# Low parts of the weights: half of the tiles on GpSimd, or all on the vector engine

## The chip, the cores and the metric

The kernel runs on one core of one Trainium2 chip. The metric is device microseconds of one execution, from the chip's own timer; several executions are given by their median.

## What is computed

One step of a hybrid decoder layer on a prompt of 2048 tokens and a sample group of 8 x 8 tokens with the same weights, all in float32. From the reference, cut:

```python
h = rmsnorm(x, norm1_g)
proj = h @ w_in                                   # 1024 -> 36 x 128 columns
q, ka, va, rw, gates = jnp.split(proj, [...], axis=-1)
att = attn_fn(q, ka, va)                          # window 128, sinks, bias
rw_out = rwkv7_mixer(rw, ...)                     # matrix state, token by token
g_a, g_b = jnp.split(jax.nn.sigmoid(gates), 2, axis=-1)
x = x + (g_a * (att @ w_pa) + g_b * (rw_out @ w_pb)) @ w_o
ug, uv = jnp.split(rmsnorm(x, norm2_g) @ w_up, 2, axis=-1)
x = x + (jax.nn.gelu(conv3(ug)) * uv) @ w_down    # inner width 2816
```

## The kernel before

**Products in two parts.** A float32 product is made of three matmuls in the faster type fp32r: each operand is split into a high part (the value cast to fp32r) and a low part (the value minus the high part), and high x high, high x low and low x high are summed in PSUM. `gemm` (L471 on) does this for one 128-column block of the weights: for each of 8 (or 4, 6) row blocks k the pairs (whi, xh), (whi, xl), (wlo, xh).

**The weights.** `load_w` loads a tile of 128 x 8 x 128 raw weights by a DMA on SP's queue (L358). `split_w` makes its parts in two halves: ScalarE (ACT) casts a half to `whi` (L383), then `wsub` (L424) subtracts it into `wlo`. `wsub` numbers its calls and sends every second one to GpSimd (POOL), the others to the vector engine (DVE). Since a tile has two halves, its first goes to DVE and its second to POOL. Raw, high and low tiles take turns in one ring of 7 buffers (`W_SLOTS`), three to a tile, so weights are made about two tiles ahead.

**First phase** (`phase1`, to about 1450 us): the tokens in six groups of up to 384. Each group runs 36 blocks of `w_in`, and attention and the RWKV scan as background processes between the blocks. The first three groups split `w_in` tiles and write the parts back to memory (L369), a third of the tiles in each; later passes load the parts (L353). So three groups make 72 tiles, 144 halves. In `gemm`, the halves of a coming tile are issued after k = 1 and k = 5 (`W_AT`). The lane solve (L1032, L1034) is a chain of 60 small DVE operations per group. The order of PE's instructions is written out by hand here, from a model of the time; the order of the other queues is left to the framework's scheduler.

**Second phase** (`phase2`): three groups of 704 tokens, each in two chunks of 352 columns. Per group: `w_ab` and `w_o` (8 tiles each), then the FFN in four parts of 4, 6, 6 and 6 blocks: up-projections (`w_ug`, `w_uv`, one tile each a block), and 8 tiles of `w_down` a part. That is 276 tiles, 552 halves. All queues, PE's too, are ordered by the scheduler, which weighs instructions by costs of its own. L1320 and L1323 make low parts of activations on DVE; L1386 and L1449 are POOL's products and sums of activations; L1333 sums squares; L1339, L1381, L1382 and L1397 are loads on POOL's queue.

`nopool` keeps halves off POOL at the turn of the two phases, and `last_load` ties the next POOL half behind POOL's loads of `outs`.

Of the kernel before, what the change touches and what calls it, by code (L numbers as in the profile page):

```python
# [78 lines left out]
Y_rwkv_post_1 = 1505  # L79
Y_rwkv_post_2 = 1205  # L80
W_AT = (1, 5)
W_POOL = (2, 0)
W_AHEAD, W_SPLIT, W_SLOTS = 2, 2, 7
P_SM = P_SW = P_T2 = 0
P_H = 1
# [86 lines left out]
class Build:  # L172
# [1322 lines left out]
    def run(self):  # L1495
        cfg = self.cfg
        self.pool_every = W_POOL[0]
        self.wnext = self.bg = None
# [112 lines left out]
```

## Time and profile before

| | |
|---|---|
| median of 3 runs | 3415.2 us (3404.68 to 3422.92) |
| the profiled execution, its own time | 3414.19 us |
| its span, first to last instruction | 3412.4 us |
| busy PE, DVE, ACT, POOL | 3274.9, 1941.7, 1162.7, 1106.6 us |
| mean granted PE clock | 0.975 of full speed |

The profile is of one execution. A row of the timeline gives start and length in us, engine, line, operation, what is written and read, the shape, and in brackets how long the engine sat idle before it and what ended that. A line named L424 is line 424 of the kernel. PE's matmuls overlap, so their lengths are about twice their distance.

### The profile page before, as it was taken

Reading aid. Unit: us, or ns where it says so; the run is one execution under the profiler, and the core shown is the slowest. Engines: PE = TensorE matmul, PEld = TensorE weight load, DVE = VectorE, ACT = ScalarE, POOL = GpSimd, SP = SyncE. Lnnn points to the kernel's source line nnn. Section 1 sums busy time; section 2 is a strip of 40 time slices with the busy share of each in tenths; the row PEclk is TensorE's granted clock in tenths of the full one; section 3 lists DMA queues with packets and bytes.
Section 4 is the critical chain, followed back from the end, with each engine's and each line's share of the span. In section 5 each row is a group of like instructions: output and inputs, shape, how many; then the busy total and the mean of one; then the engine's idle time right before and its main releaser. Section 6 shows DMA issues by size and latency. Waiting matters only on the chain.

```text
span 3412.4 us, 59346 instructions
## 1 busy us (share of the span) xinstructions
PE 3274.9 (96%) x23574; PEld 3124.1 (92%) x23574; DVE 1941.7 (57%) x3658; ACT 1162.7 (34%) x2370; POOL 1106.6 (32%) x1242
## 2 busy tenths in 40 slices
PE   7899999989999999899999999999999999999998
PEld 6879888878888889799999999999999999999998
DVE  6764775664664765655454465555464655564564
ACT  4444443332333333223232233332232323232232
POOL 4333432321221222152233332423243342343342
PEclk9989989899999999999999999999999999999999
DMA  5446467684565658562222224512222352222222
GB/s 174 147 142 228 162 204 240 214 267 151 195 197 191 211 181 287 170 217 68 64 70 72 67 63 130 172 59 77 70 66 72 97 181 74 63 70 73 68 69 74
DMA packets 197069, 460.22 MB, mean 135 GB/s; under 512 B 62719, under 2 KB 95111, under 8 KB 196791
## 3 DMA queue, kind: packets, MB, share of 16 engines
q1 hardware_dynamic: 169367, 396.33, 36.0%
q0 software_dynamic: 8704, 37.78, 3.3%
q10 hardware_dynamic: 18720, 22.31, 1.8%
q8 instruction: 185, 3.03, 0.4%
q14 instruction: 93, 0.76, 0.1%
HBM read 377.03 MB, written 79.31 MB: 134 GB/s over the span
## 4 chain that ended last, share of the span: by engine, by line
PE 78%; DVE 9%; DMA 6%; ACT 3%; issue 2%; POOL 2%; SPq 0%; ACTq 0%; DVEq 0%; POOLq 0%
PE acc L287 69%; PE ps L287 5%; DMA w<-w_in 2%; PE psA L287 2%; DVE LN L1034 1%; DVE TX L1032 1%; POOL wlo L424 1%; ACT whi L383 1%; PE psY L287 1%; ACT at L778 1%; DMA gates<-raw 1%; POOL th L1386 1%; DVE wlo L424 1%; DVE at L768 0%; DMA raw<-x 0%
## 5 line engine op out<-in xcount | busy, mean ns | idle before, releaser
L287 PE MATMUL acc<-A,whi 128*128 128x352 f32 x4992 | 1008.6, 323 | 3.8 <-DVE A L1320 3.1
L287 PE MATMUL acc<-h,whi 128*128 128x384 f32 (+2 forms) x3456 | 899.2, 340 | 14.3 <-DVE h L588 4.1
L287 PEld LDWEIGHTS acc<-A,whi 128*128 128x128 f32 x4992 | 837.3, 188 | 5.4 <-DVE A L1320 4.0
L424 POOL TENSOR_TENSOR wlo<-w,whi 128x512 fp32r<-128x512 f32 (+2 forms) x347 | 477.2, 1376 | 1070.4 <-ACT whi L383 977.9
L383 ACT CAST whi<-w 128x512 fp32r<-128x512 f32 (+2 forms) x696 | 373.6, 581 | 1066.9 <-PE acc L287 496.9
L287 PEld LDWEIGHTS acc<-h,whi 128*128 128x128 f32 x3456 | 621.8, 194 | 47.0 <-issue 15.1
L287 PE MATMUL acc<-A,wlo 128*128 128x352 f32 x2496 | 605.7, 324 | 0.0
L287 PE MATMUL acc<-B,whi 128*128 128x352 f32 x2880 | 582.5, 323 | 4.6 <-ACT B L1322 2.4
L287 PE MATMUL acc<-h,wlo 128*128 128x384 f32 (+2 forms) x1728 | 581.0, 336 | 1.4 <-DMA wlo<-w_in_lo 1.0
L287 PEld LDWEIGHTS acc<-B,whi 128*128 128x128 f32 x2880 | 481.9, 188 | 6.4 <-DVE B L1323 3.3
L424 DVE TENSOR_TENSOR wlo<-w,whi 128x512 fp32r<-128x512 f32 (+2 forms) x349 | 302.8, 868 | 256.8 <-ACT whi L383 244.4
L287 PEld LDWEIGHTS acc<-A,wlo 128*128 128x128 f32 x2496 | 435.4, 188 | 0.1
L287 PE MATMUL acc<-B,wlo 128*128 128x352 f32 x1440 | 350.2, 323 | 0.0
L287 PEld LDWEIGHTS acc<-h,wlo 128*128 128x128 f32 x1728 | 334.3, 193 | 15.0 <-issue 3.6
L287 PEld LDWEIGHTS acc<-B,wlo 128*128 128x128 f32 x1440 | 250.9, 188 | 0.0
L1478 DVE TENSOR_TENSOR x<-x,acc 128x352 f32<-128x352 f32 x188 | 89.3, 516 | 227.2 <-PE acc L287 227.2
L1449 POOL TENSOR_TENSOR ss<-ss,ssq 128x704 f32<-128x704 f32 x66 | 113.2, 1715 | 297.2 <-DVE ss L1448 264.0
L1437 DVE SCALAR_TENSOR_TENSOR cc<-ub,vt,cc 128x704 f32<-128x704 f32 (+1 forms) x132 | 145.9, 1105 | 37.4 <-ACT cc L1431 35.6
L1427 DVE TENSOR_TENSOR ub<-acc,ssq 128x352 f32<-128x352 f32 (+1 forms) x132 | 61.5, 507 | 117.5 <-PE acc L287 116.2
L1323 DVE SCALAR_TENSOR_TENSOR B<-ss,B 128x704 fp32r<-128x704 f32 x66 | 113.4, 1718 | 4.0 <-ACT B L1322 3.9
L1445 ACT ACTIVATE ss<-cc 128x704 f32<-128x704 f32 x66 | 52.4, 793 | 162.4 <-DVE cc L1437 110.5
L619 ACT COPY raw<-acc 128x384 f32<-128x384 f32 (+1 forms) x84 | 37.4, 445 | 168.4 <-PE acc L287 164.1
(302 smaller groups left out, 3605.9 us busy)
## 6 DMA issues: line engine op xcount, KB each, us to landing
whi<-w_in_hi SPq DMA_DIRECT2D x144, 512.0 KB, 4.6
wlo<-w_in_lo SPq DMA_DIRECT2D x144, 512.0 KB, 3.9
w<-w_in SPq DMA_DIRECT2D x72, 512.0 KB, 4.5
w<-w_ug SPq DMA_DIRECT2D x66, 512.0 KB, 3.5
w<-w_uv SPq DMA_DIRECT2D x66, 512.0 KB, 3.5
w<-w_down SPq DMA_DIRECT2D x72, 384.0 KB, 3.1
w_in_hi<-whi SPq DMA_DIRECT2D x36, 512.0 KB, 2.7
w_in_lo<-wlo SPq DMA_DIRECT2D x36, 512.0 KB, 5.3
```

Of the source, the lines that this page charges most:

```text
L287: self.pe(self.nc.tensor.matmul(out, lhsT, rhs, start=start, stop=stop), max(n * (1 if rhs.dtype == F32R else 4) / 2.4, 25))
L383: nc.scalar.copy(out=hi[:, a:b], in_=w[:, a:b])
L424: i = eng.tensor_tensor(**kw)
L619: nc.scalar.copy(out=raw[:, 1:1 + n], in_=acc[:, :n])
L778: nc.scalar.activation(out=t[:, h, :], in_=t[:, h, :], func=AF.Exp, bias=nm[:, h:h + 1], accum_out=su[:, h:h + 1])
L1032: nc.vector.tensor_tensor(out=tv, in0=LN[:NL, j:j + 1, j + 1:32].broadcast_to([NL, j, w]), in1=LN[:NL, 0:j, j:j + 1].broadcast_to([NL, j, ...
L1323: nc.vector.scalar_tensor_tensor(out=lo[:, :T], in0=src[:, :T], scalar=scale, in1=hi[:, :T].bitcast(F32), op0=MUL, op1=SUB)
L1427: nc.vector.tensor_tensor(out=ub[:, 2 + a:2 + e], in0=pp[:, :e - a], in1=rs[:, a:e], op=MUL)
L1437: nc.vector.scalar_tensor_tensor(out=cc[:, :n], in0=ub[:, j:j + n], scalar=self.v(wn, f), in1=cc[:, :n], op0=MUL, op1=ADD)
L1445: nc.scalar.activation(out=s[:, :T], in_=cc[:, :T], func=AF.Square, scale=GELU_A)
L1449: nc.gpsimd.tensor_tensor(out=s[:, :T], in0=s[:, :T], in1=rs[:, :T], op=MUL)
L1478: nc.vector.tensor_tensor(out=x2[m][:, a:b], in0=x2[m][:, a:b], in1=pp[:, :b - a], op=ADD)
```

## The change

The period with which halves go to POOL becomes 2^30 in place of 2, so that none does.

```diff
 W_AT = (1, 5)
-W_POOL = (2, 0)
+W_POOL = (1 << 30, 0)
 W_AHEAD, W_SPLIT, W_SLOTS = 2, 2, 7
```

The first number is `pool_every` in `wsub`; the second isn't used:

```python
eng = self.nc.gpsimd if self.wn % self.pool_every == 0 and not self.nopool else self.nc.vector
i = eng.tensor_tensor(**kw)
if eng is self.nc.gpsimd and self.last_load:
    self.tc.add_manual_dep(i.ins, self.last_load, ORDER, reason="loads first")
```

Since no half is on POOL, the tie to `last_load` falls away too. ACT's casts, the loads and the matmuls are the same.

## Rows read from the trace of the kernel before

**Rows 1.** The page, busy us of each engine, share of the span, instructions.
```profile
PE 3274.9 (96%) x23574; PEld 3124.1 (92%) x23574; DVE 1941.7 (57%) x3658; ACT 1162.7 (34%) x2370; POOL 1106.6 (32%) x1242
```
**Rows 2.** PE's waits, whole span: us in total, times, longest.
```profile
PE psA L287 <- DVE at L806: 14.6, 9, 5.2
...
PE ps L287 <- DVE G L1004: 7.0, 4, 3.3
PE acc L287 <- DVE ssq L1333: 7.0, 2, 3.8
...
PE acc L287 <- ACT B L1322: 2.4, 1, 2.4
...
PE acc L287 <- DVE wlo L424: 0.3, 2, 0.2
```
**Rows 3.** Busy time by stretch: start:end, length; PE, PEld, DVE, ACT, POOL; clock, DMA.
```profile
150.00:180.00 30.00, 24.57 (x132) 23.98 (x131) 28.62 (x86) 11.15 (x28) 6.85 (x6) 0.89 0.52 165
...
1600.00:1800.00 200.00, 200.00 (x1239) 200.00 (x1238) 109.38 (x142) 61.80 (x101) 66.33 (x59) 1.00 0.22 65
...
2110.00:2117.00 7.00, 6.93 (x27) 6.90 (x28) 2.77 (x16) 0.00 (x0) 0.00 (x0) 0.51 0.22 75
...
2400.00:2600.00 200.00, 200.00 (x1252) 200.00 (x1252) 98.13 (x131) 57.11 (x93) 64.83 (x54) 1.00 0.23 69
```
**Rows 4.** Groups by line and shape: count, busy us, mean ns, idle before them.
```profile
L424 POOL TENSOR_TENSOR wlo<-w,whi 128x512 fp32r<-128x512 f32 x251 | 370.8, 1477 | 724.7 <-ACT whi L383 684.7 <-ACT vt L723 14.4 <-DMA w_in_lo<-wlo 10.4
...
L424 DVE TENSOR_TENSOR wlo<-w,whi 128x512 fp32r<-128x512 f32 x253 | 239.4, 946 | 195.4 <-ACT whi L383 183.6 <-ACT vt L723 7.7 <-PE acc L287 1.8
...
L1323 DVE SCALAR_TENSOR_TENSOR B<-ss,B 128x704 fp32r<-128x704 f32 x66 | 113.4, 1718 | 4.0 <-ACT B L1322 3.9
...
L424 POOL TENSOR_TENSOR wlo<-w,whi 128x384 fp32r<-128x384 f32 x72 | 88.2, 1226 | 262.8 <-ACT whi L383 210.4 <-DVE x L1478 44.0 <-PE acc L287 8.4
```
**Rows 5.** The tile wlo: ns min/median/max, first and last start, main forms.
```profile
L424 POOL TENSOR_TENSOR wlo<-w,whi x347: 732/1313/2292, 18.7 to 3375.8; 128x512 fp32r<-128x512 f32 x126, 128x384 fp32r<-128x384 f32 x36, 128x256 fp32r<-128x256 f32 x12
```
**Rows 6.** Timeline of DVE, then of POOL, second phase, 1669 to 1681 us.
```profile
1669.13 0.43 DVE L424 TENSOR_TENSOR wlo<-w,whi 128x256 fp32r<-128x256 f32 x1 [1.64 <-ACT whi L383]
...
1678.81 0.69 DVE L424 TENSOR_TENSOR wlo<-w,whi 128x512 fp32r<-128x512 f32 x1 [3.56 <-ACT whi L383]
...
1679.44 1.29 POOL L424 TENSOR_TENSOR wlo<-w,whi 128x512 fp32r<-128x512 f32 x1 [4.91 <-ACT whi L383]
```
**Rows 7.** Timeline of DVE, then of POOL, in the first group's lane solve.
```profile
161.33 0.40 DVE L1034 TENSOR_TENSOR LN<-LN,TX 96x234 f32<-96x234 f32 x1
161.76 1.38 DVE L1032 TENSOR_TENSOR TX<-LN 96x238 f32<-96x238 f32 x1
...
161.51 1.36 POOL L424 TENSOR_TENSOR wlo<-w,whi 128x512 fp32r<-128x512 f32 x1 [3.86 <-ACT whi L383]
```
**Rows 8.** Timeline of POOL, then of DVE, before PE's stop at 2182 us.
```profile
2178.36 1.27 POOL L424 TENSOR_TENSOR wlo<-w,whi 128x512 fp32r<-128x512 f32 x1 [0.71 <-ACT whi L383]
2179.60 2.11 POOL L1386 TENSOR_TENSOR th<-th 128x704 f32<-128x704 f32 x1
...
2182.57 0.89 DVE L1323 SCALAR_TENSOR_TENSOR B<-th,B 128x704 fp32r<-128x704 f32 x1 [2.38 <-ACT B L1322]
```
**Rows 9.** Timeline of DVE at 66 us, first group.
```profile
66.56 0.69 DVE L424 TENSOR_TENSOR wlo<-w,whi 128x512 fp32r<-128x512 f32 x1 [3.76 <-ACT whi L383]
67.17 2.04 DVE L1004 TENSOR_TENSOR G<-ps,ct 128x512 f32<-128x512 f32 x4
```
**Rows 10.** The tile wlo on PE from 1660 to 1692 us (columns as rows 5).
```profile
L287 PE MATMUL acc<-A,wlo x20: 322/324/325, 1682.7 to 1691.6; 128*128 128x352 f32 x20
```
**Rows 11.** Timeline of POOL and DVE at a group end, then of DVE at the end.
```profile
2108.00 1.27 POOL L424 TENSOR_TENSOR wlo<-w,whi 128x512 fp32r<-128x512 f32 x1 [4.93 <-ACT whi L383]
...
2108.59 1.42 DVE L1333 TENSOR_TENSOR ssq<-ssq,ss 128x704 f32<-128x704 f32 x1 [0.52 <-ACT ss L1332]
...
3382.44 0.89 DVE L1333 TENSOR_TENSOR ssq<-ssq,ss 128x704 f32<-128x704 f32 x1 [0.92 <-ACT ss L1332]
```

## The prediction

> **What bounds the kernel now.** I read the busy times first: TensorE (PE) is busy 96% of the span, the vector engine (DVE) 57%, GpSimd (POOL) 32% [rows 1]. So the next question was what PE waited for. All of PE's idle time is 137.5 us (3412.4 - 3274.9), in many small pieces, and the reader is to see in the waits how little of it comes from what the change touches: low parts made by DVE ended 0.3 us of PE's waits in the whole span, and none made by POOL stands in that list [rows 2]. The larger pieces are DVE results of other kinds: the scores' mask L806, the masked products L1004, the sums of squares L1333 [rows 2]. Last the busy time by stretch: in the second phase PE doesn't stop for whole stretches, 200.00 of 200 us at full clock [rows 3]. There the floor is PE's own pace.
>
> **What is taken away and what is added.** POOL makes 251 halves of 128x512 and 72 of 128x384 [rows 4], 347 in all [rows 5]; the other 24 are of 128x256. All go to DVE. Alone, a DVE half takes 0.69 us for 512 columns and 0.43 us for 256 [rows 6]; for 384 I take 0.56, midway. The sum: 251 x 0.69 + 72 x 0.56 + 24 x 0.43 = 173.2 + 40.3 + 10.3 = 224 us more on DVE.
>
> Part of it comes back, because DVE is slow beside POOL. A product in the lane solve takes 0.40 us on DVE; the one that starts 0.25 us after a POOL half takes 1.38 us, and ends just after that half's 1.36 us are over [rows 7]. So a POOL half costs a busy DVE some 1.0 us, and an idle one nothing: 0 to 347 us in all. Between these ends I take what the two groups lose that lose most: DVE's own halves of 512, 253 x (0.946 - 0.69) = 65 us [rows 4, 6], and the activations' low parts L1323, 66 x (1.718 - 0.89) = 55 us [rows 4, 8]. Some of these 120 us belong to other POOL work, and other groups lose a little too. DVE then has 1942 + 224 - 120 = 2046 us, 60% of the span; from end to end 1819 to 2166 us, 53% to 63%. POOL falls from 1107 to about 630 us. Over the span no end of this makes DVE the bound; what counts is where PE stands behind DVE.
>
> **On PE's path, first phase.** Only the first three groups of tokens split weights; later ones read the parts back. DVE's fullest stretch is 150 to 180 us, the lane solve of the first group: 28.62 of 30 us [rows 3]. At its end PE waits 5.2 us for L806 [rows 2], which stands in DVE's queue behind the chain. Three POOL halves fall in the stretch, of which the rows show one, each costing the chain about 1.0 us [rows 7]; as DVE halves each costs 0.6 to 0.7. Gain 3 x 0.35 = 1 us, and about as much over the second and third group's lane solve together, where fewer halves fall.
>
> The Trainium skill, Perfetto Trace Analysis, "Optimizing Scalar/DVE Operations", holds that work may go to GpSimd where DVE is saturated, though between these two engines, which share a port, it "might not help". Taken for this full stretch, moving three halves back would add 3 x 0.69 = 2 us to the chain where the sum has a gain of 1: 3415 us by the page, by an estimate. The measured 1.38 us speaks for the page's second half, so its first changes no chance here. The page SBUF — State Buffer, "SBUF: two separate sides", names the reason: the shared port pair is an exclusive lock, and the second comer "fully blocks". The same row agrees.
>
> Against the gain stands a place such as 66 us: DVE sat idle 3.76 us in front of a half until its cast was there, with four L1004 queued behind it [rows 9], and PE waited 3.3 us for them [rows 2]. If the second half now stands ahead of them too, they come 0.6 to 0.7 us later. I allow three such places, 2 us lost. No new wait is added for the cast: DVE already waited for each tile's first one, the second ends some 0.5 us after it, and the half takes 0.69. First phase: -2 + 2 = 0, from -6 to +8, since I can't see the new order of DVE's queue.
>
> **Second phase.** Here halves are early. At the first up-projection after a w_down part, one of the tight places when halves and matmuls are counted off in their order, DVE's half ends at 1679.50 and POOL's at 1680.73 [rows 6], and the first matmul that reads that low part starts at 1682.7 [rows 10]. With both on DVE the second ends near 1680.1. This cover is 3 us for the first half and more for the second; a queue that held them back longer would cost PE the excess. The raw tile is freed 0.6 us earlier, so SP's next load can start sooner: worth 0, since no matmul waits for a weight here.
>
> PE's few stops are at group ends. Twice it waits for L1333, 7.0 us in all [rows 2]; the last L1333 takes 1.42 us beside a POOL half, 0.89 without [rows 11]. Behind a second DVE half it starts 0.1 us later: gain 0.4 each, 0.8 us. At 2182 PE waits 2.4 us for an activation's cast [rows 2], which waits for POOL's sum L1386, which stood behind a POOL half of 1.27 us [rows 8]. With POOL free the sum starts 1.1 us sooner: gain 1 us. POOL's DMA issues of outs, gates and x stood behind halves too and can go out sooner, but their buffers are still freed by DVE: 0. Two small stops of the same kind I put at 1 us. Second phase: -2.8, from -5 to +3.
>
> **PE's pace.** The same 352-column matmuls run at 1239 in 200 us in one stretch and at 1252 in another, PE busy all through and the clock full: 161.4 and 159.7 ns each [rows 3]. No wait explains the step. There are 11,808 of them, so one pace throughout against the other is 11,808 x 1.7 ns = 20 us. The profiled run had about a third at the slow pace, all those up to its first group end. I can't tell what sets it, so it stays where it is: 0, from -7 to +13 us.
>
> **The sum.** The profiled execution took 3414.2 us, 1.8 more than its span and 1.0 less than the median of 3415.2. 3414.2 + 0 - 2.8 + 0 = 3411.4; put back to the median, 3412.4. I forecast 3412 us: no change that can be seen, since about 0.5% (17 us) is what a measurement of this kernel tells from no change. The three ends on each side seldom come together; by the root of their squares (10 and 16 us) this case reaches from 3402 to 3428.
>
> **Rivals.**
> *Slower: second halves delay the DVE work that PE waits for.* The mechanism is that of 66 us, in the first three groups, where weights come just in time and 72 second halves enter DVE's queue. If all landed ahead of something that PE waits for, it would be 72 x 0.65 = 47 us; with half of them, 23 us, which gives 3437 us. Half-clock stretches come on top: after the first stop for L1333 the clock was 0.51 from 2110 to 2117 [rows 3]. It decides from some 26 such places on (17 / 0.65). Against it: apart from the lane solves DVE isn't full, and the contention saved works the other way.
>
> *Faster: the contention was what made DVE late.* L806, L1004, L1333 and the cast at 2182 are 31 us of PE's waits together [rows 2]. If half went, 15 us, and half as much again in half-clock stretches that no longer follow them, it is some 22 us: 3392 us. For it: 1.0 us for each POOL half in the full stretch [rows 7]. Against it: the chain in front of L806 stays, and L1004 waited for a late weight, not for POOL [rows 9].
>
> *The change doesn't do what it says:* a half's running number never is a multiple of 2^30, so it does; it gets no chance.
>
> **Chances.** Forecast 0.68, slower rival 0.16, faster rival 0.16; so within 0.5% 0.68, faster 0.16, slower 0.16. For 8 in 10 the range goes a little way toward each rival: 3396 to 3433.
>
> **What will show it.** Right: no half on POOL; DVE halves of 512 near 0.69 us on the mean, L1323 near 0.9 wherever L1449 isn't beside it; DVE near 2046 us busy; PE idle 130 to 140 us; the last L1333 of a group at 0.89. Wrong: waits of PE on L424, L1004 and L806 that sum to 10 us more (slower rival), or PE idle below 115 us (faster rival). If PE's idle time and the low-clock stretches stay and the time still differs, the count of matmuls in a full stretch of 200 us tells whether it is the pace.

## The result, and the profile after

The changed kernel takes 3375.3 us (median of 6 executions, 3367.5 to 3385.0), the kernel before 3409.7 in the same comparison (6 executions). The ratio is 0.990, with a 95% interval of 0.987 to 0.993: **1.0% faster**, some 34 us. The forecast of 3412 was wrong, its range (3396 to 3433) missed the time, and the rival that came nearest, the faster one, was priced too low (3392).

The profiled execution took 3380.3 us with a span of 3378.5. Busy times, to set beside [rows 1]:

```profile
PE 3266.5 (97%) x23574; PEld 3121.5 (92%) x23574; DVE 1984.5 (59%) x4005; ACT 1165.8 (35%) x2370; POOL 634.0 (19%) x895
```

No half is on POOL, as forecast, but DVE rose by 43 us only, not by 104. PE's idle time went from 137.5 to 112.0 us (3378.5 - 3266.5), past the mark of 115 that the prediction had set for the faster rival. PE's waits, to set beside [rows 2] (us in total, times, longest):

```profile
PE psA L287 <- DVE at L806: 11.5, 9, 2.3
...
PE ps L287 <- ACT BT L1014: 6.8, 13, 2.2
PE ps L287 <- DVE G L1004: 6.8, 4, 2.0
...
PE acc L287 <- DVE ssq L1333: 2.7, 2, 1.7
...
PE acc L287 <- DVE B L1323: 0.3, 1, 0.3
...
PE acc L287 <- DVE wlo L424: 0.2, 1, 0.2
```

L806, L1004, L1333 and the cast L1322, 31.0 us before, are 21.0 us now; the cast has left the list. Before, the list also had 9.8 us for L1014 (now 6.8), 4.1 for L588 (1.8) and 2.1 for L1323 (0.3). The gain is in many small pieces.

Three terms make up the 33.9 us between the two spans (3412.4 and 3378.5):

| | before | after | difference |
|---|---|---|---|
| PE idle, us | 137.5 | 112.0 | -25.5 |
| time lost to half clock (granted 0.5), by an estimate: (1 - mean granted clock) x span, us | 0.025 x 3412.4 = 85 | 0.021 x 3378.5 = 71 | -14 |
| matmuls of the second phase at the slow pace: their excess, us | 7.2 (4,303 of 11,808) | 12.9 (7,709) | +5.7 |

The last row needs a word, because all readings of the second phase below use it. From the trace I took the distance between the starts of neighbouring 352-column matmuls. At full clock it is 160.0 or 161.7 ns on the mean, in stretches of thousands of matmuls. The excess over 160.0 of the slow stretches is "the pace"; it is subtracted wherever a second phase is given "without the pace". Two windows of the kernel after show both paces (columns as [rows 3]):

```profile
1600.00:1800.00 200.00, 200.00 (x1239) 200.00 (x1238) 99.47 (x164) 54.55 (x93) 19.00 (x22) 1.00 0.23 69
2200.00:2400.00 200.00, 200.00 (x1257) 199.78 (x1256) 116.19 (x188) 66.38 (x106) 26.11 (x30) 1.00 0.22 66
```

**Where the time lies.** The first group of tokens went from 292.8 to 277.1 us, the rest of the first phase from 1163.8 to 1149.1, the second phase without the pace from 1948.7 to 1939.4. The first group ends here where the second group's first product starts, the first phase where the first 352-column matmul starts. Each row is read from one profile of its kernel. All kernels of the study, read in the same way:

| kernel | ratio to before (95%) | first group | first phase | second phase without the pace | slow matmuls |
|---|---|---|---|---|---|
| before | | 292.8 | 1456.6 | 1948.7 | 4,303 |
| after | 0.990 (0.987 to 0.993) | 277.1 | 1426.2 | 1939.4 | 7,709 |
| after, again (e11) | 0.990 (0.988 to 0.993) | 277.6 | 1426.7 | 1936.4 | 7,712 |
| first phase only (e1) | 0.995 (0.994 to 0.997) | 276.8 | 1434.2 | 1949.3 | 3,283 |
| second phase only (e2) | 0.995 (0.994 to 0.997) | 291.6 | 1449.4 | 1940.3 | 3,613 |
| after, POOL reads high part (e3) | 1.009 (1.007 to 1.012) | 296.5 | 1471.4 | 1974.3 | 2,154 |
| after, POOL reads raw and high (e4) | 1.036 (1.033 to 1.038) | 304.7 | 1477.7 | 2054.8 | 1,464 |
| before, halves exchanged (e5) | 0.996 (0.994 to 0.998) | 291.2 | 1447.6 | 1941.0 | 3,673 |
| after, raw tile held longer (e6) | 0.996 (0.994 to 0.998) | 283.4 | 1444.5 | 1945.0 | 2,059 |
| before, eight buffers (e7) | 0.989 (0.987 to 0.992) | 285.2 | 1432.7 | 1935.6 | 303 |
| before, 8 halves moved (e8) | 0.998 (0.996 to 1.000) | 291.6 | 1448.7 | 1949.7 | 3,523 |
| after, eight buffers (e9) | 0.985 (0.983 to 0.987) | 269.1 | 1420.8 | 1930.7 | 3,919 |
| before, square first (e10) | 0.997 (0.996 to 0.999) | 295.0 | 1450.3 | 1945.8 | 5,771 |
| after, POOL copies (e12) | 1.003 (1.001 to 1.005) | 291.1 | 1454.1 | 1954.7 | 5,930 |
| after, 8 halves on POOL (e13) | one run | 284.9 | 1443.1 | 1940.6 | 5 |
| before, 17 halves moved (e14) | one run | 282.8 | 1437.4 | 1954.4 | 6,894 |
| after, POOL fills (e15) | 0.994 (0.992 to 0.996) | 277.4 | 1434.2 | 1950.3 | 2 |
| before, w_ab halves moved (e16) | 0.998 (0.996 to 1.000) | 292.0 | 1446.4 | 1940.6 | 20 |

The first group can be read to some 3 us: 291.6 to 295.0 in four kernels whose first group is that of before (before, e2, e10, e16), 276.8 to 277.6 in three whose first group is that of after. The second phase is 1948.7 to 1954.4 in four kernels with all its halves split between the engines (before, e1, e8, e14), 1936.4 to 1940.6 in four without a half on POOL there (after, e11, e2, e13). So the first group gives 16 us and the second phase 11. The rest of the first phase is 1154 to 1164 us in the kernels with the first group of before and 1149 to 1158 in those with that of after: some 6 us that the spread hardly separates.

### The profile page after: what moved, and what is told of

Same layout as the page of the kernel before. It is cut to its first block, busy times and chain, and to the rows that moved or that the text cites. A ratio compares the mean times of both kernels' runs of the same rounds, so it can differ in the third digit from the quotient of the medians.

```text
span 3378.5 us, 58769 instructions
## 1 busy us (share of the span) xinstructions
PE 3266.5 (97%) x23574; PEld 3121.5 (92%) x23574; DVE 1984.5 (59%) x4005; ACT 1165.8 (35%) x2370; POOL 634.0 (19%) x895
## 4 chain that ended last, share of the span: by engine, by line
PE 83%; DVE 8%; DMA 4%; ACT 2%; issue 1%; POOL 0%; SPq 0%; DVEq 0%; ACTq 0%; POOLq 0%
PE acc L287 74%; PE ps L287 6%; PE psA L287 2%; DVE wlo L424 1%; DMA w<-w_in 1%; DVE LN L1034 1%; DVE TX L1032 1%; DMA w<-w_ab 1%; PE psY L287 1%; ACT whi L383 1%; DMA w<-w_down 0%; PE ps L290 0%; ACT at L778 0%; DVE XV L1165 0%; DVE at L768 0%
## 5 line engine op out<-in xcount | busy, mean ns | idle before, releaser
L424 DVE TENSOR_TENSOR wlo<-w,whi 128x512 fp32r<-128x512 f32 (+2 forms) x696 | 487.7, 736 | 180.0 <-ACT whi L383 168.9
L1435 POOL COPY carry<-ub 128x2 f32<-128x2 f32 x66 | 36.7, 556 | 956.1 <-DVE ub L1427 956.1
L1437 DVE SCALAR_TENSOR_TENSOR cc<-ub,vt,cc 128x704 f32<-128x704 f32 (+1 forms) x132 | 122.2, 926 | 7.5 <-ACT cc L1431 5.7
L1446 DVE SCALAR_TENSOR_TENSOR ss<-ss,cc 128x704 f32<-128x704 f32 x66 | 58.9, 892 | 59.0 <-ACT ss L1445 59.0
```

The costliest lines, as they stand in the source:

```text
L424: i = eng.tensor_tensor(**kw)
L1435: nc.gpsimd.tensor_copy(out=carry[:, f, :], in_=ub[:, n:n + 2])
L1437: nc.vector.scalar_tensor_tensor(out=cc[:, :n], in0=ub[:, j:j + n], scalar=self.v(wn, f), in1=cc[:, :n], op0=MUL, op1=ADD)
L1446: nc.vector.scalar_tensor_tensor(out=s[:, :T], in0=s[:, :T], scalar=1.0, in1=cc[:, :T], op0=ADD, op1=MUL)
```

## Experiments

**One phase at a time.** In `wsub`, halves up to number 144 are those of the first phase:

```diff
-        eng = self.nc.gpsimd if self.wn % self.pool_every == 0 and not self.nopool else self.nc.vector
+        eng = self.nc.gpsimd if self.wn % 2 == 0 and self.wn > 144 and not self.nopool else self.nc.vector    # e1
+        eng = self.nc.gpsimd if self.wn % 2 == 0 and self.wn <= 144 and not self.nopool else self.nc.vector   # e2
```

> Halves of the first phase (numbers 1 to 144) all on DVE, those of the second phase alternate as before. The profiles put 30 of the 34 us gained into the first phase, 16 of them into the first group of tokens. If that place is right, whatever the cause: 25 to 32 us faster than before, ratio 0.991 to 0.993, first group near 277 us long, phase 2 as long as before. Rival, the gain is spread over the whole span and the first phase only happened to show it in one profile: ratio 0.996 to 1.000.

> The other part alone: halves of the second phase all on DVE, those of the first phase alternate. If the gain is in the first phase: 3 to 6 us faster than before (ratio 0.998 to 0.999), first group near 293 us long, and PE idle in the second phase about 10 us less than before. Rival, the second phase gains as much as the first: ratio near 0.995, 15 us.

Both are 0.995, some 16 us each, and add up to the change. My split (30 us and 4) was read from one pair of profiles, in which the second phase's gain was half hidden by the pace: 1955.8 to 1952.3 us as it stands, 1948.7 to 1939.4 without the pace. The table's two columns then agree with e1 and e2: one phase has the gain, the other hasn't.

**POOL's old load put back.** DVE makes all halves; POOL does something of the same size beside each second half:

```diff
         i = eng.tensor_tensor(**kw)
+        if self.wn % 2 == 0 and not self.nopool:
+            k = kw["in1"].shape[1]                          # e3: high - high; e4: raw - high
+            self.nc.gpsimd.tensor_tensor(out=self.scr[:, :k], in0=kw["in1"], in1=kw["in1"], op=SUB)
```

> The changed kernel, and beside each second half POOL subtracts the same half of the high part from itself into a scratch tile that nobody reads: POOL has its old work back in size and time, but makes no low part and holds no raw tile. Theory contention (POOL's two-input instructions stop DVE's, and stop POOL's own other work): the gain goes, and since DVE keeps its 224 us of added halves the time comes to between before and 15 us above it, 3400 to 3425 us, first group 290 us or more. Theory early release of the raw tile, or theory new order of DVE's queue alone: the gain stays, 3370 to 3385 us, first group near 278.

> As the run before it, but POOL's idle subtraction reads the raw half and the high half, as the old one did, so the raw tile is also held until POOL has read it. Against the run in which POOL reads the high part only: theory contention says the same within 5 us; theory early release of the raw tile says 10 to 25 us slower than that run, most of it in the first group, where weights come just in time.

In e3 the gain goes and more with it: 3444.7 us, above the range of the contention theory. The dummy meets DVE's second half itself, so DVE's halves of 512 take 1.02 us on the mean where they take 0.81 in the changed kernel. In e4 the raw tile is held until POOL has read it, and the time is 3532.5 us, 88 above e3 where I had 10 to 25. That was the first sign that the raw tile's stay matters, and in the second phase above all (80 of the 88 us), where I had put it at nothing. It isn't all release: e4's dummy of 512 columns is also longer than e3's, 1.66 us on the mean against 1.41. SP's queue shows the release (us in total, times, longest), in the kernel before, then in e4:

```profile
SPq L358 <- POOL wlo L424: 297.3, 255, 8.9
```

```profile
SPq L358 <- POOL scr L427: 135.7, 136, 2.9
```

The load of the next raw tile waits for POOL 255 times in the kernel before and 136 times in e4; in the one after it has no half of POOL's to wait for.

**The raw tile's release.** e5 exchanges the two halves of a tile; e6 lets POOL hold the raw tile of the changed kernel a little longer with short copies; e7 and e9 add a buffer to the ring, to the kernel before and to the changed one:

```diff
+        eng = self.nc.gpsimd if self.wn % 2 == 1 and not self.nopool else self.nc.vector                  # e5
+        self.nc.gpsimd.tensor_copy(out=self.scr[:, 0, :1], in_=kw["out"][:, 0, :1].bitcast(F32))          # e6
+        self.nc.gpsimd.tensor_copy(out=self.scr[:, :1], in_=kw["in0"][:, :1])                             # e6
-W_AHEAD, W_SPLIT, W_SLOTS = 2, 2, 7
+W_AHEAD, W_SPLIT, W_SLOTS = 2, 2, 8                                                                       # e7, e9
```

> The kernel before with the two halves of a tile exchanged: POOL makes each first half, DVE each second. POOL and DVE do as much as before and meet as often, but POOL starts one cast (0.5 us) earlier, so the raw tile is free about as early as in the changed kernel. In the second phase the profiles so far, with the slow pace of PE's matmuls taken out, give 1949 us with halves on POOL (two kernels) and 1940 us without (two kernels). Theory early release (SP's next load starts sooner, so casts, halves and the ACT work behind the casts come sooner): 1940 to 1944 us in the second phase, 5 to 9 us faster than before. Theory contention (DVE and POOL block each other): 1947 to 1951 us, and the time within 4 us of before.

> The changed kernel, and behind each second half POOL copies one element a row of the low part and then 128 columns of the raw half into a scratch tile that nobody reads: the raw tile stays taken for some 0.5 us longer, while POOL's work is short (one read, 128 columns). Theory early release: what the second phase gained goes, 1946 to 1952 us with the pace taken out, and L1333 makes PE wait over 3 us at a group's end again; 8 to 12 us slower than the changed kernel. Theory contention: within 3 us of the changed kernel, 1938 to 1943 us.

> The kernel before with 8 buffers in the weights' ring in place of 7 (to make room, one of 8 small buffers of the softmax is given up): the next raw load need not wait for the release of the last raw tile. POOL keeps its halves. Theory early release: the second phase gains 9 us or more (1940 us or less with the pace taken out) and the time is 9 to 20 us shorter than before. Theory contention: POOL's halves still meet DVE, the second phase stays at 1946 to 1950 us, and the time within 4 us of before.

> The changed kernel (no half on POOL) with 8 buffers in the weights' ring; one of 8 small softmax buffers is given up as in the run with 8 buffers and POOL's halves. With a spare raw buffer the next load waits no more for the last raw tile's release, so what is left between these two kernels is contention and POOL's own queue. Theory that the change worked only by the earlier release: the two are the same within 5 us, 3373 to 3383 us. Theory that contention is worth something of its own: 10 to 25 us faster than the one with POOL's halves, 3353 to 3368 us, the first group near 272 to 278 us in place of 285, and the lane solve's operations at 0.4 us.

e7 is the clearest: with POOL's halves in place, one more buffer gives as much as the change (0.989, and 13 us in the second phase). So the making of weights was on PE's path, through the ring: in the second phase SP's next load leaves 0.03 us (median, from the trace) after the last raw tile is released, in the kernel before as in the one after. From the start of a tile's first cast to the next load it takes 2.6 us on the median (3.2 on the mean) in the second phase of before, e1 and e8, and 2.3 (2.5) after. e7 doesn't keep all of the contention: the halves meet less often there, and DVE's own of 512 take 0.83 us on the mean where they take 0.95 before.

e9 shows that this is not all. With the spare buffer the release no longer holds up the next load, and the change still gives some 15 to 18 us (0.985 of before where e7 has 0.989): the first group is another 16 us shorter and the second phase 5, and the rest of the first phase takes 4 back. e5 gave the number that early release asked for in the second phase (1941.0), but not by the release: its DVE halves of 512 take 1.27 us beside POOL's, and from first cast to next load it takes 2.6 us on the median (3.1 on the mean), as before. What moved is POOL's queue, where halves start one cast earlier; the last experiments show that to be worth something by itself. e6 costs some 20 us against the changed kernel (0.996 for 0.990), twice what I had, with 6 us in the first group, 12 in the rest of the first phase and 7 in the second phase, of which the pace gives 9 back; its L1333 stops did not come back but vanished, so the sign that I had named for early release failed.

**The lane solve.** The prediction had put the first phase's gain there. e8 moves the 8 halves from 133 to 171 us to DVE, e13 leaves only these on POOL, e14 moves the 17 before them:

```diff
+        eng = self.nc.gpsimd if self.wn % 2 == 0 and not 36 <= self.wn <= 50 and not self.nopool else self.nc.vector   # e8
+        eng = self.nc.gpsimd if self.wn % 2 == 0 and 36 <= self.wn <= 50 and not self.nopool else self.nc.vector       # e13
+        eng = self.nc.gpsimd if self.wn % 2 == 0 and self.wn > 34 and not self.nopool else self.nc.vector              # e14
```

> The kernel before with only 8 of the 347 halves moved to DVE: those that POOL made from 133 to 171 us, around the first group's lane solve. The first group was 293 and 292 us long with halves on POOL and 277 us without. Theory that the lane solve carries the first group's gain (chain blocked by five halves, L806 waiting behind it, half clock behind that stop): first group 282 to 285 us, the stop at L806 1 to 2 us. Theory that the gain is made of many small stops all over the group (L1004, POOL's own products standing behind halves): 288 to 291 us.

> The opposite of the run in which only 8 halves moved: those 8, made from 133 to 171 us around the first group's lane solve, stay on POOL and all others are on DVE. If the lane solve has no share in the first group's gain, as that run said: first group 276 to 280 us. If the two parts cover for each other (either of them late keeps the end late): 283 to 290 us.

> The kernel before with only the first 17 of POOL's halves moved to DVE, those up to 128 us. Theory that the first group's gain comes from many small stops before the lane solve (L588, L1004, L1014, POOL's L982) and is kept afterwards: first group 284 to 288 us. Theory that a gain before the lane solve is lost in it, since five halves still block its chain: 290 to 295 us, with the lane solve's chain starting some 5 us sooner and PE's stop for L806 longer than 5 us.

In the first group e8 alone gives about 1 us, e14 alone 10. But put back last, the same 8 halves cost 8 us (e13), and PE waits 5.9 us for L806 again. (e13 and e14 are single runs.) The two places cover for each other, so neither run alone gives the share of its place. DVE, then POOL, in e13's lane solve, to set beside [rows 7]:

```profile
157.08 0.40 DVE L1034 TENSOR_TENSOR LN<-LN,TX 96x240 f32<-96x240 f32 x1
157.52 1.51 DVE L1032 TENSOR_TENSOR TX<-LN 96x238 f32<-96x238 f32 x1
159.06 0.40 DVE L1034 TENSOR_TENSOR LN<-LN,TX 96x238 f32<-96x238 f32 x1
...
157.48 1.29 POOL L424 TENSOR_TENSOR wlo<-w,whi 128x512 fp32r<-128x512 f32 x1 [5.06 <-DVE LN L1034]
```

From first to last operation the chain takes 33.1 us here, 33.2 before, 30.4 after. It starts at 139 to 140 us in e13, e14 and after, and at 147 before. The 3 us of the length are contention in the chain, as far as these pairs go: e8, which has no half of POOL's in it either, takes 32.1 us. The 8 us of the start follow the making of weights: with eight buffers and all of POOL's halves (e7) the chain starts at 136 us, with the raw tile held longer (e6) at 145.

**Contention or POOL's queue.** In the changed kernel POOL is given 1.3 us of work beside each second half once more, now without holding the raw tile: two copies of one operand (e12), or a copy of one element a row and two fills (e15):

```diff
+            for _ in range(2): self.nc.gpsimd.tensor_copy(out=self.scr[:, :k], in_=kw["in1"])    # e12
+            self.nc.gpsimd.tensor_copy(out=self.scr[:, 0, :1], in_=kw["in1"][:, 0, :1])          # e15
+            for _ in range(2): self.nc.gpsimd.memset(self.scr[:, :k], 0.0)                       # e15
```

> The changed kernel, and beside each second half POOL copies the same half of the high part twice into a scratch tile that nobody reads: one operand, some 0.65 us each, 1.3 us together, so POOL's queue is taken for as long as by the old half, no raw tile is held, and the two operands that the old half read at once are gone. For the first group, 277 us long in three kernels without halves on POOL, 292 to 295 with them, and 297 with a two-operand dummy. Theory contention (two-operand work of POOL stops DVE): first group 275 to 281 us, DVE's halves of 512 at 0.70 to 0.75 us, the time within 6 us of the changed kernel. Theory POOL's own queue (its products, stored sums and copies stand behind halves): first group 285 to 293 us, and the time 10 to 20 us above the changed kernel.

> The changed kernel, and beside each second half POOL copies one element a row of the high part and then fills a scratch tile twice (128x512, some 0.55 us each): POOL's queue is taken for some 1.3 us in the old half's place and time, but it reads next to nothing. Beside copies (the run before) DVE's chain operations went from 0.4 to 0.65 and 0.85 us; if fills do the same, DVE's halves of 512 are near 0.92 us again and the run tells nothing more. If DVE is left alone by fills (halves at 0.70 to 0.75 us), the two theories part: POOL's own queue says first group 285 to 292 us and 10 us or more above the changed kernel; contention says first group 276 to 280 us and within 5 us of the changed kernel.

e12 missed: copies block DVE as well, so the run couldn't tell the theories apart. e15 did. The lane solve beside POOL, DVE and then POOL, first in e12 and then in e15 (the lines of these kernels lie 3 and 5 below those of before):

```profile
162.38 0.40 DVE L1035 TENSOR_TENSOR TX<-LN 96x234 f32<-96x234 f32 x1
162.81 0.85 DVE L1037 TENSOR_TENSOR LN<-LN,TX 96x234 f32<-96x234 f32 x1
...
162.80 2.27 POOL L427 COPY scr<-whi 128x512 f32<-128x512 f32 x2 [4.13 <-ACT whi L383]
```

```profile
157.22 0.39 DVE L1039 TENSOR_TENSOR LN<-LN,TX 96x234 f32<-96x234 f32 x1
157.53 0.68 DVE L424 TENSOR_TENSOR wlo<-w,whi 128x512 fp32r<-128x512 f32 x1
158.14 0.39 DVE L1037 TENSOR_TENSOR TX<-LN 96x228 f32<-96x228 f32 x1
...
157.40 1.11 POOL L429 MEMSET scr<- 128x512 f32 x2
```

Beside a fill DVE's operations keep their 0.39 and 0.68 us; beside a copy one takes 0.85. And with fills the first group is 277.4 us, the whole gain kept, while the second phase is 1950.3, the whole gain lost. In the first group the copies and fills of e15 take 57 us of POOL, no less than the 52 us of the old halves. So **the first group's gain doesn't come from POOL's queue: it is contention** (POOL's halves blocking DVE, which makes weights and the lane solve late), with the release that e6 priced at 6 us in it. Nor does it come from the new order of DVE's queue alone, since e3 keeps every half on DVE and loses the gain. And **POOL's own queue is enough to undo the second phase's gain**, though e15 leaves the earlier release (2.3 us from cast to load on the median) and DVE's speed (0.80 us for a half of 512) as they are after the change. The Trainium skill, SBUF — State Buffer, "Who interferes with whom", draws the line at the same place: an operation of DVE with two SBUF inputs contends with a GpSimd operation that reads SBUF, not with one that only writes it. The two runs agree with it, 0.85 us beside a read and 0.39 beside a fill.

**Where in the second phase.** POOL's sums L1386 feed ACT's cast L1322, and that cast feeds the products of w_o. Groups by form, the cast's count and busy time, then its idle time and what ended it, in the kernels before, after, e15 (where L1386 and L1322 are L1391 and L1327) and e16:

```profile
L1322 ACT ACTIVATE B<-th 128x704 fp32r<-128x704 f32 x24 | 19.0, 793 | 76.1 <-POOL th L1386 75.9
```

```profile
L1322 ACT ACTIVATE B<-th 128x704 fp32r<-128x704 f32 x24 | 19.0, 793 | 32.6 <-POOL th L1386 32.6
```

```profile
L1327 ACT ACTIVATE B<-th 128x704 fp32r<-128x704 f32 x24 | 19.0, 793 | 71.8 <-POOL th L1391 71.8
```

```profile
L1322 ACT ACTIVATE B<-th 128x704 fp32r<-128x704 f32 x24 | 19.0, 792 | 52.8 <-POOL th L1386 52.8
```

ACT's idle time alone is no cost: e7 has 130.9 us in this row and the second shortest second phase of all. What counts is how late the sums are. From the trace, the 24 sums start 43 us in all after the products L1385 that they add are done, 10 in the kernel after, 45 in e15 and 25 in e16. Of all kernels here, those with 25 to 31 us (e16, e5) have second phases near 1941 us, those with 41 us or more 1945.8 and up, those with less than 14 us 1945.0 and down.

In the kernel before a sum is late mostly in two ways: by 0.9 to 1.7 us behind a half's own work, and by 3.6 to 4.5 us, three times, behind a half that still waits for ACT's cast of a weight. The stop at 2182 us [rows 8] began so 30 us before; ACT, DVE, then POOL:

```profile
2151.07 1.14 ACT L383 CAST whi<-w 128x512 fp32r<-128x512 f32 x2 [5.12 <-DMA w<-w_ab]
...
2147.50 1.80 DVE L1385 SCALAR_TENSOR_TENSOR th<-th,acc 128x352 f32<-128x352 f32 x4
...
2152.30 1.28 POOL L424 TENSOR_TENSOR wlo<-w,whi 128x512 fp32r<-128x512 f32 x1 [3.88 <-ACT whi L383]
2153.54 1.71 POOL L1386 TENSOR_TENSOR th<-th 128x704 f32<-128x704 f32 x1
```

The sum's products are done at 2149.3, and it starts at 2153.5, behind the half. From there on each sum, ACT's cast of it, L1323 and the next products follow one another without a pause, with some 1.0 us of a half in every round, until PE stops. e16 takes only the halves of the w_ab tiles off POOL, the ones that stand in front of these sums:

```diff
-            hi, lo = self.weights("w_ab", m)
+            self.nopool = True; hi, lo = self.weights("w_ab", m)
```

> The kernel before with only the second halves of the w_ab tiles moved to DVE: 8 tiles in each of three groups of the second phase, 23 of POOL's 347 halves. Theory that the second phase's gain sits at this one stage, where POOL's sums L1386 stand behind halves and the casts of these tiles stand in front of L1332: most of the 10 us, second phase at 1939 to 1943 us with the pace taken out (1949 before, 1938 with all halves moved), PE's stops for L1322 and L1323 under 1 us together, the time 6 to 10 us below before. Theory that the gain is spread over the second phase's 276 tiles: a twelfth of it, 1947 to 1950 us.

With these 23 of 347 halves moved the second phase is 1940.6 us, 8 to 10 of the 11, and the stops for L1322 and L1323 fall from 4.5 to 0.6 us. The whole time says less: 0.998 is some 8 us, and up to 7 of them can be the pace (20 slow matmuls in place of 4,303). The run shows the place; these halves also stop meeting DVE and holding raw tiles there, so the mechanism rests on e15.

**The stop at L1333.** ACT, then DVE, at the first group end of the kernel before (its L1333 is in [rows 11]), then of the one after:

```profile
2106.73 1.14 ACT L383 CAST whi<-w 128x512 fp32r<-128x512 f32 x2 [4.39 <-DMA w<-w_ab]
2107.78 0.79 ACT L1332 ACTIVATE ss<-x 128x704 f32<-128x704 f32 x1
```

```profile
2073.92 1.14 ACT L383 CAST whi<-w 128x512 fp32r<-128x512 f32 x2 [3.74 <-DMA w<-w_ab]
2074.97 0.79 ACT L1332 ACTIVATE ss<-x 128x704 f32<-128x704 f32 x1
...
2075.79 0.89 DVE L1333 TENSOR_TENSOR ssq<-ssq,ss 128x704 f32<-128x704 f32 x1
```

The square L1332 has its input some 3 us earlier, but stands in ACT's queue behind two casts that wait for a load. PE's wait is put down to L1333; the wait under it is for a weight. e10 gives ACT the square first, in the kernel before:

```diff
-            nc.scalar.copy(out=hi[:, a:b], in_=w[:, a:b])
+            cast = nc.scalar.copy(out=hi[:, a:b], in_=w[:, a:b])
+            self.tie and self.tc.add_manual_dep(cast.ins, self.tie, ORDER, reason="square first")
...
+            self.tie = self.sq_ins if g and m == 2 else None; hi, lo = self.weights("w_ab", m); self.tie = None
```

> The kernel before, and at each of the two turns between groups of the second phase ACT makes the last square (L1332) ahead of the casts of the third w_ab tile. Only ACT's order, and DVE's behind it, changes there; halves, contention and releases stay. Theory that PE's wait for L1333 is a wait for a weight's load (the square stood in ACT's queue behind a cast that waited for its raw tile): the two stops of 3.2 and 3.8 us go to under 0.7 us each, the second phase to 1939 to 1943 us with the pace taken out, the time 6 to 10 us shorter than before. Theory that the stop is L1333's own contention with POOL (1.42 us in place of 0.89): the stops stay above 2.5 us and the time within 2 us of before.

```profile
2098.02 0.79 ACT L1332 ACTIVATE ss<-x 128x704 f32<-128x704 f32 x1 [2.43 <-DVE x L1478]
2099.92 1.14 ACT L383 CAST whi<-w 128x512 fp32r<-128x512 f32 x2 [1.11 <-DMA w<-w_ab]
...
2098.84 0.89 DVE L1333 TENSOR_TENSOR ssq<-ssq,ss 128x704 f32<-128x704 f32 x1 [0.92 <-ACT ss L1332]
```

The stops fall from 3.2 and 3.8 to 1.4 and 0.4 us, so the reading holds, though the first stays above the 0.7 us that I had as the most. The second phase takes 1945.8 us, between the two theories' numbers: a new stop of 1.8 us for L1385 and waits for L1322 of 3.5 us in place of 2.4 took part of it back, and POOL's sums stayed late (47 us). These stops alone don't make the second phase: e13 and e16 still have 5.8 and 4.9 us of L1333, and both take 1940.6 us.

**The same kernel again.**

> The changed kernel once more, with nothing altered, for the spread between two profiles of one program: first group 277 us long within 1.5 us, second phase 1939 to 1941 us with the pace taken out, 0.988 to 0.993 of before in time. The share of its matmuls at the slow pace (7,709 of 11,808 in the first profile) is left open: if the pace belongs to the program it comes again, if not it differs by thousands.

All readings repeat; the second phase without the pace, 1936.4, lies 3 us below the first profile's and so gives the spread of that column.

## Why the prediction was wrong, point by point

**What bounds the kernel.** It was right that PE's own work does, and that its idle time is in many small pieces. The step that failed is how I read the waits: I went by the engine and line that a wait of PE is put down to. Low parts ended 0.3 us of PE's waits [rows 2], and from that I took weights to be early. But queues are in order. L1333's 7.0 us were waits for a weight's load, passed on through ACT's queue. L1322's 2.4 us go back to a half that waited 3.88 us for a weight's cast 30 us earlier, passed on through POOL's, and to the 1.0 us of a half in every round after it. The Trainium skill says in Perfetto Trace Analysis, "Tensor Engine Instruction (MATMUL, LD_WEIGHTS)", that "ACT/DVE/GPSIMD are strict FIFO"; the rows of L1332 and L1386 agree. The view that would have shown it is the chain of waits of the first 300 us alone, before and then after:

```profile
by line: DMA w<-w_in 17.3%; PE acc L287 15.1%; POOL wlo L424 5.0%; issue 4.8%; ACT whi L383 4.4%; PE ps L287 4.3%; PE psA L287 4.0%; DVE LN L1034 3.4%; DVE wlo L424 3.4%; DVE TX L1032 3.1%; DMA xr<-x 2.1%; ACT at L778 2.0%; POOL rstd L532 1
```

```profile
by line: PE acc L287 34.2%; PE ps L287 8.6%; issue 6.4%; DVE wlo L424 5.3%; DMA w<-w_in 4.3%; PE psA L287 2.9%; ACT at L778 2.9%; DVE TX L1032 2.6%; DVE LN L1034 2.4%; ACT whi L383 1.7%; DMA LN<-ln 1.7%; DMA ln<-G 1.4%; DVE at L768 1.3%; DV
```

Before, loads of weights, casts and halves were 30% of the chain (17.3 + 5.0 + 4.4 + 3.4), after 11% (4.3 + 1.7 + 5.3).

**DVE's sum.** +224 us, less 120 given back, 65 of them by DVE's own halves and 55 by L1323 B. So the halves L424 were to rise by 159 us and the rest to fall by 55. L424 rose by 185 (302.8 to 487.7, all shapes), and the rest fell by 142. L1323 B came out as forecast, 0.88 us; L1437 gave 24 us more, L1323 A 15, and many small groups the others:

```profile
L424 DVE TENSOR_TENSOR wlo<-w,whi 128x512 fp32r<-128x512 f32 x504 | 388.7, 805 | 145.1 <-ACT whi L383 134.2 <-ACT vt L723 6.5 <-PE ps L287 2.9
...
L1323 DVE SCALAR_TENSOR_TENSOR B<-ss,B 128x704 fp32r<-128x704 f32 x66 | 58.1, 881 | 1.1 <-ACT B L1322 1.1
```

Halves of 512 take 0.81 us on the mean, not 0.69, beside POOL's other work. The mechanism was right; the term that was mis-sized is what the groups other than halves get back, 142 us where I had 55.

**First phase: net 0, measured -16 for the first group and some -6 for the rest.** "Gain 3 x 0.35 = 1 us" in the lane solve was a gain per half of the right kind; five halves fell there, not three, and the chain became 2.8 us shorter. The step that failed stands beside it: that contention mattered in the lane solve alone. Where DVE isn't full it still makes the weights that PE is short of: e14 gives 10 of the 16 us with halves moved ahead of the lane solve only, e15 keeps the 16 with POOL's queue full again, and e7 shows that weights are short there (8 us). The loss of 2 us allowed for places like 66 us did show, at one place. The stop at 66 us itself went from 3.3 to 1.6 us, but at 87 us there is a new one of 1.9 us for L1004, behind two halves on DVE in the kernel after, where PE waited 1.3 us for L989 before:

```profile
84.83 1.29 DVE L424 TENSOR_TENSOR wlo<-w,whi 128x512 fp32r<-128x512 f32 x2 [0.47 <-ACT whi L383]
86.04 2.03 DVE L1004 TENSOR_TENSOR G<-ps,ct 128x512 f32<-128x512 f32 x4
```

That is 0.6 us lost, the price that I had for one place; L1004's waits together are 6.8 us after 7.0.

**Second phase: -2.8, measured -11.** Each place was named, and each was priced too low. L1333, "0.4 each": 3.2 and 3.8 us became 1.0 and 1.7 (2.6 and 0.7 in e11), through the load rather than through the 1.42 us. L1322 at 2182, "1 us": all 2.4 went. "Two small stops, 1 us": L1323's 2.1 us became 0.3. "The raw tile is freed 0.6 us earlier ... worth 0, since no matmul waits for a weight here" is the sentence that e7 refutes, by 13 us of gain, and e4 by most of its 80 us of loss. Release and POOL's queue are both in the 11 us, and no run here shares them out: e6 prices a longer hold at 7 us, e15 a full queue at 11.

**Pace.** Left at 0, from -7 to +13: it was +5.7, inside.

**Rivals.** The faster one had the right mechanism for the first group, where contention carries most of the 16 us; in the second phase the gain came through POOL's queue and the ring, which it doesn't name. It took half of 31 us of stops and half as much for the clock, 22 us. The four lines gave 10 us, lines that I hadn't listed the other 15, and the half clock 14. The slower one, second halves ahead of work that PE waits for, showed in the 1.9 us at 87 us, far from the 26 places that it needed. Its 0.16 was as large as the faster one's for no better reason than that I couldn't see the new order.

## What to carry to other kernels

Before calling a transfer or an early step hidden, follow PE's waits one step further down, through the instruction that stood ahead on the same engine: a late load can hide behind a square, a sum or a cast that was ready. Where tiles go round in a ring with only one spare, a few tenths of a microsecond in the last reader of a tile can come back in many loads; one buffer more tells how much (here 35 us by the means, and 53 together with the change: 3356.8 us, 0.985 of before, the fastest kernel of this study). Work given to a second engine cost twice here, by blocking the first where both read the same memory and by standing in its own queue ahead of other work; filling and copying dummies separate the two.

## What the runs showed of the hardware that I had not expected

**The pace belongs to the program.** The second phase of the changed kernel had 7,709 matmuls at 161.7 ns in one profile and 7,712 in another, changing pace at the same places. Of 11,808 matmuls other kernels had between 2 and 6,894 at that pace, while the matmuls were the same. That is up to 13 us, so times of kernels that differ by less can't be compared without it; what sets it stays open.

**Fills by POOL leave DVE alone, copies don't.** The chain's operations take 0.39 us beside a fill and 0.65 to 0.85 beside a copy of one operand. In the other direction, POOL's copies of one element a row took from 0.18 to 1.33 us in e15's lane solve, with DVE busy all through, while its fills of 512 kept to 0.53 us on the mean.
